# VectorE's instructions of the state space stage in the order of the kernel's calls

## The chip, the cores and the metric

The kernel runs on one core of one Trainium2 chip. TensorE (PE in the profile) multiplies, VectorE (DVE), ScalarE (ACT) and GpSimd (POOL) do the element-wise work, and transfers are issued from the SyncE queue (SP). The metric is device time in microseconds; lower is better. A difference of less than about 0.2% (5 us) cannot be told from no change here.

## The reference

One layer of a hybrid decoder on 1024 tokens of width 1024: token mixing (stick-breaking attention beside a Mamba-2 mixer), cross-attention into 256 memory tokens, and a SwiGLU feed-forward. Float32 data are carried as a high and a low part, and a product is three matmuls (high x high, high x low, low x high). The part that matters here is the state space mixer, in chunks of 128 tokens, with 32 heads in 4 groups:

```python
cb = einsum('bclgn,bcsgn->bcgls', cc, bc)
y_diag = einsum('bcgls,bcgels,bcsgep->bclgep', cb, decay, xc)
states = einsum('bclgn,bcgel,bclgep->bcgepn', bc, decay_to_end, xc)
# scan over chunks: prev * chunk_decay + states
y_off = einsum('bclgn,bcgepn,bcgel->bclgep', cc, prev_states, exp(a_cs))
y = (y_diag + y_off + d_skip * x) * silu(z)      # then an RMS norm within each group
```

The result goes through the projection `w_br_ssm`. In the same stretch of the program the keys and values of the cross-attention are computed from the memory tokens, since nothing else depends on them yet.

## The kernel before

The kernel is written for a framework that schedules. Python calls create instructions; a planner then chooses, for each engine, the order in which that engine will run them, by the data they need and its own guess of durations. On the chip every engine runs its own list strictly from the front, and waits on semaphores of the others. So the order of calls is not the order on an engine, unless code says so. `InTurn` wraps an engine and can say so: while its `on` is set, each instruction of that engine is planned behind the one created before it. It is in use in two other stretches of the kernel (`lead_in`). In the state space stage it is off.

The stage is a loop over 32 chunk steps `n` (4 groups `g` of 8 chunks `c`), preceded by two steps that only prepare. In one turn of the loop the calls are, in this order:

- `prep(n + 2)`: every fourth chunk `open_four` splits B and C (tiles `bl`, `cl` on VectorE, L122) and masks their product (`cb`, L1114). Then for the chunk: two matmuls into `dec` (L1137), two exponentials on ScalarE (L1138), one wide multiply by `cb` on VectorE (tile `seg`, L1139), and the weighted x: a multiply on GpSimd (L1144), its high part on ScalarE and its low part on VectorE (`s2r`, L122).
- `branch_load`: in four of the eight steps of a group, a block of `w_br_ssm` is scaled and split (VectorE's part is L1237, twice).
- `branch`: 12 matmuls of the output projection into a bank `mm`, added to `acc` by VectorE (tile `a`, L1250; ScalarE copies instead for the first group). Up to two of these in a step.
- `states(n + 1)`: three matmuls into `pst`; GpSimd decays the old state (L1161), VectorE adds `pst` (L1162), ScalarE takes the high part `sth`, VectorE the low part `stl` (L122).
- `outp(n)`: GpSimd multiplies x by `dsk` (L1178); three matmuls of C with the state into `po`; VectorE scales `po` (L1183); GpSimd adds it to y (L1184); 16 small matmuls, in two halves, into `pd` (L1191); VectorE adds `pd` (L1194) and multiplies by z (L1195); ScalarE squares (L1198), GpSimd makes the reciprocal root (L173, L174), ScalarE scales (L1200).
- `flip(n - 2)`: four transposes into `ptr` (L1213), ScalarE takes the high part (L1216), VectorE the low part `otl` (L1217).

Between these calls `mem_work` spreads the memory work (64 small pieces) over the first eight turns: 16 weight blocks are loaded and split (VectorE's part is tile `bw`, L122, 128x1024), and the matmuls of a block come after the load of the block two ahead. Room for the split blocks is two tiles `bw` of two blocks each, so the fifth block waits until the products of the first two are done.

PSUM has one bank each for `pst`, `po`, `pd` and `ptr`, and two each for `dec` and `mm`: TensorE can run about one step ahead of VectorE and no further.

Of the kernel before, what the change touches and what calls it, by code (L numbers as in the profile page):

```python
# [54 lines left out]
def hybrid_block(ctx, tc, a, out, dbg=None):  # L55
    nc = tc.nc
    V, A, T = [InTurn(tc, e) for e in (nc.vector, nc.scalar, nc.tensor)]
# [12 lines left out]
    def mk(pl, shape, dt, tag, bufs=None):  # L70
        uid[0] += 1
        kw = {} if bufs is None else {"bufs": bufs}
        return pl.tile(shape, dt, tag=tag, name=f"{tag}_{uid[0]}", **kw)
# [50 lines left out]
    def mm3(ps, sh, sl, mh, ml, start, stop):  # L124
        first = T.matmul(ps, sh, mh, start=start, stop=False)  # L125
        T.matmul(ps, sh, ml, start=False, stop=False)  # L126
        T.matmul(ps, sl, mh, start=False, stop=stop)  # L127
        return first
# [874 lines left out]
    with ExitStack() as p3:  # L1003
# [146 lines left out]
        def states(n):  # L1150
            g, c = divmod(n, NCH)
            d, gd = chk[n], grp[g]
            if c == NCH - 1:
                return
            pst_ = mk(ps, [P, HALF], F32, "pst")
            marks.append(mm3(pst_, d["bh"], d["bl"], d["xwh"], d["xwl"], True, True))
            state = mk(gb, [P, HALF], F32, "state")
            if c == 0:
                A.activation(state, pst_, AF.Copy)
            else:  # L1160
                G.tensor_tensor(v3(state), v3(gd["state"]), bc(cdm, c, g), ALU.mult)  # L1161
                V.tensor_tensor(state, state, pst_, ALU.add)  # L1162
            gd["state"] = state
            sth = mk(gb, [P, HALF], F32R, "sth")
            stl = mk(gb, [P, HALF], F32R, "stl")
            hi_sb(sth, state, "a")
            lo_of(stl, state, sth)
            gd["st", c + 1] = (sth, stl)
# [34 lines left out]
        def flip(n):  # L1203
            g, c = divmod(n, NCH)
            half, ci = divmod(c, 4)
            gd = grp[g]
            if ci == 0:
                gd["oh", half] = mk(ot, [P, 4, HALF], F32R, "oth")
                gd["ol", half] = mk(ot, [P, 4, HALF], F32R, "otl")
            y = chk[n]["y"]  # L1210
            pt = mk(ps, [P, 4, P], F32, "ptr")
            for k in range(4):
                T.transpose(pt[:, k, :], y[:, k * P:(k + 1) * P], ident)  # L1213
            sl = slice(ci * P, (ci + 1) * P)
            oh = gd["oh", half][:, :, sl]
            A.activation(oh, pt, AF.Copy)  # L1216
            V.tensor_tensor(gd["ol", half][:, :, sl], pt, oh.bitcast(F32), ALU.subtract)  # L1217
# [7 lines left out]
        def branch_load(g, fh, kk):  # L1225

            if (g, fh) not in brw:
                brw[g, fh] = halves()
            w = brw[g, fh]
            raw = mk(wr, [P, 2, HALF], F32, "wraw")  # L1230
            r0 = g * HALF + kk * 2 * P
            nc.sync.dma_start(raw, a["w_br_ssm"][0][r0:r0 + 2 * P, fh * HALF:(fh + 1) * HALF].rearrange("(k p) f -> p k f", p=P))
            for j in range(2):
                k = 2 * kk + j
                gain = pcol("g_ssm_norm", g * 4 + k)
                A.activation(w[:, k, 0], raw[:, j], AF.Copy, scale=gain)
                V.scalar_tensor_tensor(w[:, k, 1], raw[:, j], gain, w[:, k, 0].bitcast(F32), ALU.mult, ALU.subtract)  # L1237

        def branch(g, half, f):
            oh, ol = grp[g]["oh", half], grp[g]["ol", half]  # L1240
            sl = slice(half * HALF, (half + 1) * HALF)
            w = brw[g, f // 4]
            fs = slice(f % 4 * P, (f % 4 + 1) * P)
            pb = mk(ps, [P, HALF], F32, "mm", bufs=2)
            for k in range(4):
                mm3(pb, w[:, k, 0, fs], w[:, k, 1, fs], oh[:, k, :], ol[:, k, :], k == 0, k == 3)
            if g == 0:
                A.activation(acc[f][:, sl], pb, AF.Copy)
            else:
                V.tensor_tensor(acc[f][:, sl], acc[f][:, sl], pb, ALU.add)  # L1250
# [4 lines left out]
        def mem_quanta():  # L1255
# [63 lines left out]
            for i, ps_ in enumerate(parts):  # L1319
                if i + 2 < len(loads):  # L1320
                    yield loads[i + 2]
                yield from ps_

        for n in range(AHEAD):
            prep(n)
        mq = list(mem_quanta())
# [2 lines left out]
        def mem_work(upto):  # L1329
            while mq and NQ - len(mq) < upto:  # L1330
                mq.pop(0)()
# [8 lines left out]
        for n in range(-AHEAD, NN + 2):  # L1340
            if AHEAD <= n + AHEAD < NN:
                prep(n + AHEAD)
            mem_work((n + AHEAD) * NQ / MEM_SPAN)
            for l in loads.pop(n, []):
                branch_load(*l)
            if todo and todo[0][0] <= n:
                todo.pop(0)[1]()
            if 0 <= n + 1 < NN:
                states(n + 1)
            mem_work((n + AHEAD + 0.33) * NQ / MEM_SPAN)  # L1350
            if 0 <= n < NN:
                outp(n)
            mem_work((n + AHEAD + 0.67) * NQ / MEM_SPAN)
            if todo and todo[0][0] <= n:
                todo.pop(0)[1]()
            if 0 <= n - 2 < NN:
                flip(n - 2)
                if (n - 2) % 4 == 3:
                    g, c = divmod(n - 2, NCH)
                    fs = list(range(KT)) if c == 3 else list(range(4, KT)) + list(range(4))  # L1360
                    todo += [(n + 2, lambda g=g, hf_=c // 4, f=f: branch(g, hf_, f)) for f in fs]

# [889 lines left out]
```

## Time and profile before

| | |
|---|---|
| median of 3 runs | 2514.5 us (2513.93 to 2516.95) |
| the profiled execution | 2516.72 us, of which the span is 2515.0 us |
| busy: TensorE, VectorE, ScalarE, GpSimd | 2449.4, 1803.6, 1161.5, 720.2 us |
| state space stage | from about 1086.6 to 1411 us of the span |
| in it, busy: TensorE, VectorE | 311.12 and 281.58 of 324.40 us |

An engine that is busy throughout sets the time of its stretch, if its work is not itself stretched by waits; here TensorE is nearly always busy, and VectorE is nearly so in the early part of the stage. Timeline rows give the start, the duration, the engine, the line and the operation, and in brackets the idle time just ahead and what ended it. An instruction of VectorE shows some 0.08 us more than the distance to the start of the next, since two of them overlap at their ends.

### The profile page before, as it was taken

The numbers are of one execution on the slowest core, as the hardware profiler recorded it, in microseconds if no ns is written. First come the engines' busy times: TensorE is split into PE (matmuls) and PEld (weight loads), VectorE is DVE, ScalarE is ACT, GpSimd is POOL, SyncE is SP. The second block draws the span as 40 slices with busy tenths as digits, with TensorE's granted clock in tenths as the row PEclk, the third lists the DMA queues.
The fourth block names the chain that finished last, engine by engine and source line by source line (L and its number), as shares of the span: only waits on it lengthen the run. The fifth ranks groups of instructions, "written<-read, shape, count | busy, mean of one in ns | idle before, by whom it ended". The sixth has DMA issues, their size and how long they took to land. (4 is left out here: it accounts for less than half of the span.)

```text
span 2515.0 us, 33312 instructions
## 1 busy us (share of the span) xinstructions
PE 2449.4 (97%) x12306; PEld 2016.7 (80%) x12306; DVE 1803.6 (72%) x2205; ACT 1161.5 (46%) x2054; POOL 720.2 (29%) x581
## 2 busy tenths in 40 slices
PE   7999999999999999999999999999999999999998
PEld 5788888888877888877777787887888888888887
DVE  7665777767587878689888674577368665666997
ACT  5333455555555665566644312344335333344433
POOL 3221545443111111146666241104011332220001
PEclk9999999999999999999999999999999999999999
DMA  7431443333534343366333481322142322234322
GB/s 248 157 118 49 138 145 107 109 101 93 160 97 109 95 117 91 94 191 206 98 100 88 136 273 64 131 94 67 67 151 63 101 80 76 93 98 165 131 101 101
DMA packets 249132, 295.62 MB, mean 118 GB/s; under 512 B 17023, under 2 KB 169096, under 8 KB 248842
## 3 DMA queue, kind: packets, MB, share of 16 engines
q1 hardware_dynamic: 248682, 292.45, 36.9%
q8 instruction: 97, 1.59, 0.3%
q10 hardware_dynamic: 288, 1.05, 0.1%
q14 instruction: 65, 0.53, 0.1%
HBM read 202.20 MB, written 74.45 MB: 110 GB/s over the span
## 5 line engine op out<-in xcount | busy, mean ns | idle before, releaser
L911 DVE TENSOR_TENSOR_SCAN n<-n,mask 128x128 f32<-128x128 f32 (+7 forms) x128 | 189.8, 1510 | 23.7 <-ACT n L910 22.4
L122 DVE TENSOR_TENSOR sw<-sf,sw 128x512 fp32r<-128x512 f32 x142 | 129.5, 916 | 69.6 <-ACT sw L119 67.6
L119 ACT ACTIVATE sw<-sf 128x512 fp32r<-128x512 f32 x142 | 88.9, 628 | 155.8 <-PE mm L230 139.2
L928 ACT ACTIVATE wth<-tr,mone 128x512 fp32r<-128x512 f32 x192 | 110.7, 585 | 83.6 <-PE tr L925 81.7
L929 DVE SCALAR_TENSOR_TENSOR wtl<-tr,wth 128x512 fp32r<-128x512 f32 x192 | 99.7, 544 | 48.6 <-ACT wth L928 48.6
L693 DVE SCALAR_TENSOR_TENSOR b<-b,prmT,b 128x1023 f32<-128x1023 f32 (+2 forms) x72 | 109.7, 1523 | 16.9 <-ACT b L687 16.3
L196 POOL TENSOR_TENSOR sf<-wr,wr 128x512 f32<-128x512 f32 x36 | 51.8, 1438 | 232.7 <-DMA wr<-in_w_gu_dram 95.1
L122 DVE TENSOR_TENSOR sw<-wr,sw 128x512 fp32r<-128x512 f32 x107 | 100.3, 939 | 24.4 <-ACT sw L119 24.3
L229 PE MATMUL mm<-h,sw 128*128 128x512 f32 x288 | 112.0, 389 | 0.0
L230 PE MATMUL mm<-h,sw 128*128 128x512 f32 x288 | 111.7, 389 | 0.0
L228 PE MATMUL mm<-h,sw 128*128 128x512 f32 x288 | 109.9, 389 | 0.0
L910 ACT ACTIVATE n<-sc 128x512 f32<-128x512 f32 (+1 forms) x192 | 88.6, 494 | 45.9 <-PE tr L925 28.7
L173 POOL TENSOR_SCALAR rstd<-ms 128x1 f32<-128x1 f32 x74 | 29.3, 396 | 273.9 <-ACT x L180 195.0
L125 PE MATMUL mm<-oth,bw 128*128 128x512 f32 x256 | 103.7, 405 | 3.1 <-DVE a L1250 3.1
L115 POOL TENSOR_SCALAR v<-va 128x512 fp32r<-128x512 f32 x16 | 20.5, 1282 | 286.3 <-PE av L938 166.3
L127 PE MATMUL p<-bw,h 128*128 128x512 f32 x256 | 100.2, 392 | 0.5 <-DVE h L122 0.5
L127 PE MATMUL mm<-oth,bw 128*128 128x512 f32 x256 | 100.5, 393 | 0.0
L126 PE MATMUL mm<-otl,bw 128*128 128x512 f32 x256 | 100.5, 392 | 0.0
L125 PE MATMUL p<-bw,h 128*128 128x512 f32 x256 | 99.9, 390 | 0.0
L126 PE MATMUL p<-bw,h 128*128 128x512 f32 x256 | 99.8, 390 | 0.0
L925 PE MATMUL tr<-ident,n 128*128 128x128 f32 x576 | 95.5, 275 | 3.6 <-DVE wtl L929 3.6
L119 ACT ACTIVATE zh<-zr 128x512 fp32r<-128x512 f32 x72 | 45.0, 630 | 104.8 <-PE ma L492 52.4
(661 smaller groups left out, 7814.2 us busy)
## 6 DMA issues: line engine op xcount, KB each, us to landing
wr<-in_w_in_dram SPq DMA_DIRECT2D x36, 512.0 KB
wr<-in_w_gu_dram SPq DMA_DIRECT2D x72, 256.0 KB
zr<-in_w_in_dram SPq DMA_DIRECT2D x28, 512.0 KB
wraw<-in_w_in_dram SPq DMA_DIRECT2D x20, 512.0 KB
gu_d<-t SPq DMA_DIRECT2D x36, 256.0 KB
zs_d<-zo SPq DMA_DIRECT2D x32, 256.0 KB
xs_d<-b SPq DMA_DIRECT2D x32, 256.0 KB
kl<-gt SPq DMA_DIRECT2D x64, 128.0 KB
```

Of the source, the lines that this page charges most:

```text
L119: A.activation(o, i, AF.Copy)
L122: eng.tensor_tensor(o, i, hi.bitcast(F32), ALU.subtract)
L125: first = T.matmul(ps, sh, mh, start=start, stop=False)
L126: T.matmul(ps, sh, ml, start=False, stop=False)
L127: T.matmul(ps, sl, mh, start=False, stop=stop)
L228: T.matmul(ps, w[0][:, k, :], bh, start=first and k == 0, stop=False, skip_group_check=True)
L229: T.matmul(ps, w[0][:, k, :], bl, start=False, stop=False, skip_group_check=True)
L230: ins = T.matmul(ps, w[1][:, k, :], bh, start=False, stop=last and k == 3, skip_group_check=True)
L693: V.scalar_tensor_tensor(acc[:, sh:], y[:, :S - sh], cw(3 - sh, f), acc[:, sh:], ALU.mult, ALU.add)
L911: V.tensor_tensor_scan(nt[:, 0:L][:, ::-1], nt[:, 0:L][:, ::-1], mask[:, S - L:][:, ::-1], 1.0, ALU.mult, ALU.max)
L928: A.activation(wh[:, t0 * P:], pt[:, t0 * P:], AF.Identity, bias=mone)
L929: V.scalar_tensor_tensor(wl[:, t0 * P:], pt[:, t0 * P:], -1.0, wh[:, t0 * P:].bitcast(F32), ALU.add, ALU.subtract)
```

## The change

VectorE's wrapper is switched on for the whole stage. All its instructions of `prep`, `mem_work`, `branch_load`, `branch`, `states`, `outp` and `flip` now stand on VectorE in the order of the calls. Nothing is computed otherwise, and no instruction is added; the planner places the other engines' instructions anew around the fixed list.

```diff
+        V.on = True
         for n in range(AHEAD):
             prep(n)
         mq = list(mem_quanta())
...
                     todo += [(n + 2, lambda g=g, hf_=c // 4, f=f: branch(g, hf_, f)) for f in fs]
+        V.on, V.last = False, None
```

Inside the wrapper an instruction carries the wrapper's line (L49) instead of its own.

The first place is VectorE in an ordinary step of the last group, before. `s4` is the tile of `seg`, `s2_2830` the scaled `po` and `s2_2828` the y of the same chunk.

```order
L1139 SCALAR_TENSOR_TENSOR s4_2816_13323<-s4_2816_13323,cb_2768_13113 128x1024
L1250 TENSOR_TENSOR a8_2050_9940<-a8_2050_9940,mm_2822_13337 128x512
L1162 TENSOR_TENSOR state_2824_13355<-state_2824_13355,pst_2823_13351 128x512
L1183 TENSOR_TENSOR s2_2830_13370<-po_2829_13366,eam_428_2335 128x512
L122 TENSOR_TENSOR stl_2826_13359<-state_2824_13355,sth_2825_13358 128x512
L1194 TENSOR_TENSOR s2_2828_13364<-s2_2828_13364,pd_2831_13373 128x512
L1195 TENSOR_TENSOR s2_2828_13364<-s2_2828_13364,s2_2827_13362 128x512
```

The same place on VectorE now:

```order
L49 SCALAR_TENSOR_TENSOR s4_2816_13323<-s4_2816_13323,cb_2768_13113 128x1024
L49 TENSOR_TENSOR s2r_2821_13334<-s2_2819_13331,s2r_2820_13333 128x512
L49 TENSOR_TENSOR a8_2050_9940<-a8_2050_9940,mm_2822_13337 128x512
L49 TENSOR_TENSOR state_2824_13355<-state_2824_13355,pst_2823_13351 128x512
L49 TENSOR_TENSOR stl_2826_13359<-state_2824_13355,sth_2825_13358 128x512
L49 TENSOR_TENSOR s2_2830_13370<-po_2829_13366,eam_428_2335 128x512
L49 TENSOR_TENSOR s2_2828_13364<-s2_2828_13364,pd_2831_13373 128x512
L49 TENSOR_TENSOR s2_2828_13364<-s2_2828_13364,s2_2827_13362 128x512
```

`stl`, which needs ScalarE's answer to `state`, now stands directly behind `state`; the scaled `po`, to which GpSimd answers, stands behind `stl` and directly ahead of the add of `pd` that needs GpSimd's answer.

The second place is VectorE at the start of the stage, before. `bw` are the split memory weights (`bw_2097` blocks 1 and 2, `bw_2100` blocks 3 and 4, `bw_2111` block 5), `s2_2129` is the y of the first chunk.

```order
L122 TENSOR_TENSOR stl_2108_10165<-state_2106_10162,sth_2107_10164 128x512
L1139 SCALAR_TENSOR_TENSOR s4_2115_10212<-s4_2115_10212,cb_2082_10074 128x1024
L1194 TENSOR_TENSOR s2_2129_10271<-s2_2129_10271,pd_2130_10273 128x512
L122 TENSOR_TENSOR s2r_2120_10223<-s2_2118_10220,s2r_2119_10222 128x512
L1195 TENSOR_TENSOR s2_2129_10271<-s2_2129_10271,s2_2128_10269 128x512
L122 TENSOR_TENSOR bw_2100_10121<-wraw_2104_10154,bw_2100_10121 128x1024
L1162 TENSOR_TENSOR state_2122_10242<-state_2122_10242,pst_2121_10238 128x512
L122 TENSOR_TENSOR s2r_2141_10335<-s2_2139_10332,s2r_2140_10334 128x512
L122 TENSOR_TENSOR bw_2111_10196<-wraw_2112_10197,bw_2111_10196 128x1024
```

The same place on VectorE now:

```order
L49 TENSOR_TENSOR bw_2100_10121<-wraw_2104_10154,bw_2100_10121 128x1024
L49 TENSOR_TENSOR stl_2108_10165<-state_2106_10162,sth_2107_10164 128x512
L49 TENSOR_TENSOR bw_2111_10196<-wraw_2112_10197,bw_2111_10196 128x1024
L49 SCALAR_TENSOR_TENSOR s4_2115_10212<-s4_2115_10212,cb_2082_10074 128x1024
L49 TENSOR_TENSOR s2r_2120_10223<-s2_2118_10220,s2r_2119_10222 128x512
L49 TENSOR_TENSOR state_2122_10242<-state_2122_10242,pst_2121_10238 128x512
L49 TENSOR_TENSOR stl_2124_10246<-state_2122_10242,sth_2123_10245 128x512
L49 TENSOR_TENSOR bw_2111_10196<-wraw_2126_10258,bw_2111_10196 128x1024
L49 TENSOR_TENSOR s2_2129_10271<-s2_2129_10271,pd_2130_10273 128x512
```

The first half of `bw_2111`, whose room comes free only with the products of the first two blocks, has moved ahead of the third `s4`, its `s2r`, the state and the first chunk's y.

## The prediction

> **What bounds the kernel now.** I read the busy shares of the page first, then the busy time by stretches of the stage, then the timeline of one ordinary step, then VectorE's waits.
>
> ```profile
> PE 2449.4 (97%) x12306; PEld 2016.7 (80%) x12306; DVE 1803.6 (72%) x2205; ACT 1161.5 (46%) x2054; POOL 720.2 (29%) x581
> ```
>
> Over the whole program TensorE is the bound. The change touches one stage only, so the four groups of that stage are taken apart; the stretches are cut at the first chunk's end of each group. Columns: length, then busy time and instructions of TensorE, its weight loads, VectorE, ScalarE, GpSimd, then the granted clock, the DMA share and GB/s.
>
> ```profile
> 1086.60:1193.00 106.40, 99.06 (x752) 80.83 (x752) 97.34 (x104) 68.37 (x121) 62.19 (x50) 0.97 0.67 208
> 1193.00:1272.00 79.00, 77.18 (x572) 62.53 (x571) 62.84 (x78) 45.95 (x90) 49.29 (x47) 1.00 0.35 104
> 1272.00:1348.00 76.00, 74.30 (x557) 60.01 (x557) 68.34 (x90) 38.72 (x75) 45.41 (x44) 1.00 0.36 106
> 1348.00:1411.00 63.00, 60.57 (x465) 48.81 (x465) 53.05 (x73) 28.18 (x54) 33.73 (x35) 1.00 0.27 76
> 1086.60:1411.00 324.40, 311.12 (x2342) 252.18 (x2342) 281.58 (x341) 181.22 (x340) 190.62 (x174) 0.99 0.44 133
> ```
>
> In the last three groups TensorE is busy 96 to 98%, in the first (memory work) 93%, with VectorE at 91%. TensorE leaves 13.3 us of 324.4 unused, VectorE 42.8 us. So there is little to gain, and VectorE has 42.8 us to lose before it becomes the bound, as long as its waits fall where TensorE still has work.
>
> How much of that is left within a step is seen in one ordinary step, from one multiply by z to the next (VectorE), with GpSimd and TensorE beside it:
>
> ```profile
> 1376.85 0.80 DVE L1195 TENSOR_TENSOR s<-s,s 128x512 f32<-128x512 f32 x1
> ...
> 1381.64 0.68 DVE L1162 TENSOR_TENSOR state<-state,pst 128x512 f32<-128x512 f32 x1
> 1382.23 0.69 DVE L1183 TENSOR_TENSOR s<-po,eam 128x512 f32<-128x512 f32 x1
> 1383.08 0.91 DVE L122 TENSOR_TENSOR stl<-state,sth 128x512 fp32r<-128x512 f32 x1 [0.16 <-ACT sth L119]
> 1385.16 0.69 DVE L1194 TENSOR_TENSOR s<-s,pd 128x512 f32<-128x512 f32 x1 [1.18 <-PE dec L1137]
> 1385.89 0.91 DVE L1195 TENSOR_TENSOR s<-s,s 128x512 f32<-128x512 f32 x1
> ```
>
> ```profile
> 1382.39 1.04 POOL L1161 TENSOR_TENSOR state<-state,cdm 128x512 f32<-128x512 f32 x1 [2.35 <-DVE state L1162]
> 1383.40 1.73 POOL L1184 TENSOR_TENSOR s<-s,s 128x512 f32<-128x512 f32 x1
> ```
>
> ```profile
> 1380.37 1.15 PE L1191 MATMUL pd<-s,s 128*64 128x64 f32 x32
> ...
> 1389.42 0.98 PE L1191 MATMUL pd<-s,s 128*64 128x64 f32 x26
> ```
>
> TensorE's period is 1389.42 - 1380.37 = 9.05 us, VectorE's 1385.89 - 1376.85 = 9.04 us. Within it VectorE sits idle for 0.16 us ahead of `stl` and 1.18 us ahead of the add of `pd`. The row names a matmul for the second, but GpSimd's L1184 ended at 1385.13, 0.03 us before the add began, and the add reads its output: that is the true releaser. This step hides two round trips in each other. After `state`, ScalarE makes `sth`; in that time VectorE scales `po`. GpSimd then adds the scaled `po` while VectorE makes `stl`.
>
> **The change, part by part.** It removes and adds no arithmetic and no transfer. It moves instructions on VectorE, with four effects.
>
> First, the round trip to ScalarE. `stl` now stands right behind `state`. From the rows above, `state` began at 1381.64 and `stl` could begin at 1383.08, 1.44 us later, since ScalarE's part took until then. Without the 0.68 us of `state` itself, VectorE is idle for 0.76 us where it scaled `po` before. There are 24 such states.
>
> Second, the round trip to GpSimd. The scaled `po` now stands directly ahead of the add of `pd`, and nothing of VectorE lies between. The trace has this situation once, at the end of the stage:
>
> ```profile
> 1407.14 0.68 DVE L1183 TENSOR_TENSOR s<-po,eam 128x512 f32<-128x512 f32 x1
> ...
> 1407.90 1.29 POOL L1184 TENSOR_TENSOR s<-s,s 128x512 f32<-128x512 f32 x1 [1.45 <-DVE s L1183]
> ...
> 1409.22 0.69 DVE L1194 TENSOR_TENSOR s<-s,pd 128x512 f32<-128x512 f32 x1 [1.40 <-POOL s L1184]
> ```
>
> 2.08 us from start to start, and 1.40 us of it idle. There are 28 such chunks:
>
> ```profile
> L1183 DVE TENSOR_TENSOR s<-po,eam 128x512 f32<-128x512 f32 x28 | 19.1, 683 | 0.1
> L1162 DVE TENSOR_TENSOR state<-state,pst 128x512 f32<-128x512 f32 x24 | 16.3, 678 | 0.0
> ```
>
> GpSimd's add has two prices in the trace: 1.73 us at 1383.40, where `stl` ran on VectorE until 1383.99, and 1.29 us at 1407.90, where VectorE stood still. In the new order VectorE stands still during it, so I take 1.29; with 1.73 the idle time would be 1.84 us, and the sum 28 x 0.44 = 12.3 us more. The Trainium skill's page "SBUF — State Buffer", section "Who interferes with whom", says why the two may differ: a VectorE instruction with two SBUF inputs contends with a GpSimd instruction that reads SBUF, and the later one is blocked until the first is through. `stl` is such an instruction, and the rows agree in direction (0.44 us more, for 0.59 us of overlap), so by that rule too the lower price holds where VectorE waits.
>
> Put into the ordinary step: `state` to the add of `pd` took 1385.16 - 1381.64 = 3.52 us. Now it is 1.44 (state to `stl`) + 0.84 (`stl`, 0.91 us less the overlap with the next) + 2.08 = 4.36 us. The step becomes 9.04 + 0.84 = 9.88 us, above TensorE's 9.05. Here the bound changes: TensorE has one bank for each of `pst`, `po`, `pd` and `ptr`, so it can run ahead by about a step and then waits for VectorE.
>
> The stage then takes, in each group, VectorE's busy time plus the waits that it can no longer fill. A group has 7 scaled `po` and 6 added states: 7 x 1.40 + 6 x 0.76 = 14.4 us.
>
> First group: 97.34 + 14.4 = 111.7 against 106.4 us: +5.3. Second: 62.84 + 14.4 = 77.2 against 79.0; TensorE's 77.18 us of work lie under it, so I leave it at 79: 0. Third: 68.34 + 14.4 = 82.7 against 76.0: +6.7. Fourth: 53.05 + 14.4 = 67.4 against 63.0: +4.4. Together +16.4 us.
>
> Third, the other waits of VectorE. They are these now, longest total first (total, times, longest):
>
> ```profile
> DVE s L1194 <- POOL s L1184: 14.7, 11, 2.8
> DVE s L1139 <- ACT s L1138: 8.0, 9, 3.1
> DVE s2r L122 <- ACT s2r L119: 7.7, 9, 1.8
> DVE bw L122 <- ACT bw L119: 5.1, 4, 2.1
> DVE otl L1217 <- ACT oth L1216: 3.8, 4, 1.8
> DVE bw L1237 <- ACT bw L1236: 1.6, 2, 1.4
> DVE s L1194 <- PE dec L1137: 1.2, 1, 1.2
> DVE stl L122 <- ACT sth L119: 0.9, 6, 0.2
> DVE bl L122 <- ACT bh L119: 0.3, 1, 0.3
> ```
>
> The first, the seventh and the eighth (16.8 us) are the two round trips, counted above. The other six sum to 26.5 us: exponentials, high parts, weight splits. A list in fixed order cannot go round them, but the longer step also gives ScalarE and TensorE more time, and `s2r` now stands last in a step, far behind GpSimd's part. So they lie between 0 and, in the three groups where VectorE becomes the bound, three quarters of 26.5, some 20 us. I take the middle, 10 us (an estimate).
>
> Fourth, at the start the first half of `bw_2111` waits for room, until the products of the first two weight blocks are done. Behind it on VectorE stand the third `s4`, its `s2r`, `state` and `stl`, and behind those wait TensorE's `pst` and `pd`. One line of a block's products is in the groups of TensorE's instructions:
>
> ```profile
> L127 PE MATMUL mm<-mh,bw 128*128 128x256 f32 x64 | 18.5, 289 | 1.1 <-DVE bw L122 1.1
> ```
>
> A block has three such lines of 8, so at most 24 x 0.289 = 6.9 us, less what is pipelined and what VectorE's own splits ahead of it cover: between 0 and 7 us. I take it as inside the 10 us above, since TensorE is at work in that wait, and keep 5 us for the upper end.
>
> SP's and GpSimd's lists shift with the buffers that VectorE frees, but no transfer is added and the DMA share is 0.27 to 0.36 in the last three groups, so I cost that at nothing; if a load of x came late, it would show as a longer wait of GpSimd's L1144. After the stage nothing changes: the last products and adds of `branch` follow in the same order.
>
> The sum: 16.4 + 10 = +26 us on the profiled execution, 2516.7 to about 2543. That execution lies 2.2 us above the median of 2514.5 us, so the median becomes 2540.5 us.
>
> **The rivals.** *TensorE's clock falls.* When TensorE waits long enough, its next products run slower. The trace shows it once, in the first group:
>
> ```profile
> 1164.21 0.80 PE L126 MATMUL mm<-bw,mh 128*128 128x512 f32 x1 [1.78 <-DVE bw L122]
> ...
> 1165.23 0.63 PE L125 MATMUL mm<-bw,mh 128*128 128x512 f32 x1
> 1165.66 0.63 PE L126 MATMUL mm<-bw,mh 128*128 128x512 f32 x1
> ...
> 1167.72 0.39 PE L126 MATMUL mm<-bw,mh 128*128 128x512 f32 x1
> 1167.95 0.40 PE L127 MATMUL mm<-bw,mlo 128*128 128x512 f32 x1
> ```
>
> After a wait of 1.78 us the starts are 0.43 us apart instead of 0.23 for about 3 us: some 1.5 us lost beside the wait. Another wait did not do it:
>
> ```profile
> 1361.97 0.50 PE L1137 MATMUL dec<-colrows,keyrows 128*128 128x512 f32 x1 [1.29 <-ACT s L1138]
> ```
>
> So this rival decides from a single wait somewhere between 1.3 and 1.8 us. Against it: an ordinary step makes TensorE wait 9.88 - 9.05 = 0.83 us. For it: steps with `open_four` or `branch_load` put three to four more instructions on VectorE's list, and what TensorE waits for them comes in one piece. Once in each of the 24 steps with a state it costs 24 x 1.5 = 36 us on top of 26: about 2576. The Trainium skill's page "TensorE: Matmul & The Clock Gate", section "What's actually happening", has a stricter rule: the half clock comes after at least one idle window of about 3.4 us. By that rule hardly any step would fall into it and the sum would stay at 26 us; the row above shows it after a shorter single wait, and the row decides.
>
> *Faster: the call order stops VectorE from running ahead.* In the first group the planner lets VectorE split weights and prepare `bl` and `cl` of later chunks before work that TensorE needs; TensorE then stood idle for 106.40 - 99.06 = 7.3 us there, and 13.3 us in the whole stage. If call order brought each TensorE input just in time, and VectorE's waits fell where it has slack, all of that could go: 2514.5 - 13 = 2501. It decides for the faster side only if the ordinary step stays at or below 9.05 us, which means that GpSimd's answer must come 0.83 us sooner than the rows say. I see nothing that would bring it.
>
> *No difference.* VectorE's 42.8 us of idle time swallow the new waits in the groups with slack, and the second group's surplus is used. It would take the 16.4 us to be no more than 5.
>
> *The change does nothing* can be left out: the lists of VectorE in both places shown differ.
>
> **How the numbers follow.** VectorE becoming the bound, with a loss of more than 5 us and up to about 55: 0.67. The clock rival: 0.11. No difference within 0.2% (5 us, what can be told here): 0.10. Faster by more than 5 us: 0.12. Slower is 0.67 + 0.11 = 0.78. The forecast's own upper end is 16.4 + 20 + 12.3 + 5 = 54 us, so 2568; its lower end is near no change. The range reaches below to 2512, which leaves most of the faster case out, and above to 2578, which takes in most of the clock case.
>
> **What would show it.** In the changed kernel's profile: the add of `pd` waiting for GpSimd's L1184, now under the wrapper's line, near 28 x 1.40 = 39 us instead of 14.7; a wait on `sth` near 24 x 0.76 = 18 us instead of 0.9; GpSimd's L1184 near 1.29 us instead of 1.73; an ordinary step in the last two groups of about 9.9 us; TensorE's idle time in the stage up by roughly the time lost, in pieces below 1.3 us. I am wrong if TensorE's step stays at 9.05 us, if GpSimd's add does not get shorter, if the six other waits grow instead of halving, or if the granted clock in the stage falls clearly below 0.99.

## The result, and the profile after

The changed kernel takes 2546.4 us (median of 4 runs, 2542.4 to 2548.5) against 2514.8 us for the kernel before (median of 4): a ratio of 1.0119, with a 95% interval from 1.0105 to 1.0133. It is slower by some 30 us; the forecast was 26. Its profiled execution took 2546.62 us, of which the span is 2544.9 us.

The page of the changed kernel, busy shares over the whole program:

```profile
PE 2453.7 (96%) x12306; PEld 2016.7 (79%) x12306; DVE 1780.5 (70%) x2205; ACT 1162.6 (46%) x2054; POOL 719.6 (28%) x581
```

VectorE is busy for 23 us less than before, in a program that is 30 us longer. The stage, cut at the same chunks as in the table of before (columns as there):

```profile
1086.60:1212.50 125.90, 107.29 (x779) 87.79 (x779) 86.78 (x101) 69.61 (x124) 57.67 (x51) 0.94 0.54 167
1212.50:1288.50 76.00, 72.56 (x546) 57.55 (x545) 57.15 (x78) 45.13 (x88) 47.08 (x45) 0.98 0.37 113
1288.50:1373.20 84.70, 75.78 (x557) 59.38 (x556) 64.93 (x91) 39.28 (x75) 45.47 (x44) 1.00 0.30 95
1373.20:1440.50 67.30, 62.13 (x459) 48.98 (x458) 50.30 (x74) 27.78 (x53) 35.86 (x35) 0.97 0.27 77
```

The groups are longer by 19.5, -3.0, 8.7 and 4.3 us, 29.5 us in all. VectorE's busy time fell from 281.6 to 259.2 us and its idle time rose from 42.8 to 94.7 us: +52 - 22.4 = 29.5. In the third group TensorE, which was idle for 1.7 us of 76.0, is now idle for 8.9 of 84.7. Over the stage TensorE's idle time rose from 13.3 to 36.1 us and its busy time from 311.1 to 317.8 us, with six matmul records fewer: 22.9 us more of waiting, and 6.6 us more for the same products at a lower granted clock (0.97 over the stage, 0.99 before).

VectorE's waits over the stage (total, times, longest):

```profile
DVE s L49 <- POOL s L1184: 40.6, 28, 1.9
DVE stl L49 <- ACT sth L119: 36.9, 24, 3.2
DVE bw L49 <- ACT bw L119: 8.0, 3, 4.1
DVE bw L49 <- ACT bw L1236: 4.6, 2, 2.4
```

The two round trips hold 77.5 of the 94.7 us. One ordinary step of the last group on VectorE, from one multiply by z to the next:

```profile
1394.56 0.80 DVE L49 TENSOR_TENSOR s<-s,s 128x512 f32<-128x512 f32 x1
...
1398.80 0.68 DVE L49 TENSOR_TENSOR state<-state,pst 128x512 f32<-128x512 f32 x1
1400.69 0.69 DVE L49 TENSOR_TENSOR stl<-state,sth 128x512 fp32r<-128x512 f32 x1 [1.21 <-ACT sth L119]
...
1403.38 0.69 DVE L49 TENSOR_TENSOR s<-s,pd 128x512 f32<-128x512 f32 x1 [1.40 <-POOL s L1184]
1404.11 0.80 DVE L49 TENSOR_TENSOR s<-s,s 128x512 f32<-128x512 f32 x1
```

The step takes 9.55 us. Both trips stand bare in it, one behind the other. The longest wait of this kind stands one step later, which has a block of `w_br_ssm` to split; VectorE's rows, then ScalarE's in the same time:

```profile
1408.36 0.67 DVE L49 TENSOR_TENSOR state<-state,pst 128x512 f32<-128x512 f32 x1
1412.21 0.69 DVE L49 TENSOR_TENSOR stl<-state,sth 128x512 fp32r<-128x512 f32 x1 [3.18 <-ACT sth L119]
```

```profile
1408.61 2.56 ACT L1236 ACTIVATE bw<-wraw,prmT 128x512 fp32r<-128x512 f32 x4 [0.19 <-PE mm L127]
...
1411.56 0.61 ACT L119 ACTIVATE sth<-state 128x512 fp32r<-128x512 f32 x1
```

The state was there from 1409.03 on, but ScalarE's own list has four weight parts and the transposed y ahead of `sth`. VectorE stands still until ScalarE gets there.

Most of the loss lies in the first group. VectorE at its start:

```profile
1104.30 1.23 DVE L49 TENSOR_TENSOR bw<-wraw,bw 128x1024 fp32r<-128x1024 f32 x1 [2.96 <-ACT bw L119]
...
1110.18 1.22 DVE L49 TENSOR_TENSOR bw<-wraw,bw 128x1024 fp32r<-128x1024 f32 x1 [4.05 <-ACT bw L119]
...
1117.35 0.68 DVE L49 TENSOR_TENSOR s<-s,pd 128x512 f32<-128x512 f32 x1
```

ScalarE's high parts that these two splits wait for, and the loads on SP's queue:

```profile
1103.21 1.06 ACT L119 ACTIVATE bw<-wraw 128x1024 fp32r<-128x1024 f32 x1 [0.48 <-DMA wraw<-in_w_xkv_dram]
...
1109.08 1.06 ACT L119 ACTIVATE bw<-wraw 128x1024 fp32r<-128x1024 f32 x1 [0.88 <-DMA wraw<-in_w_xkv_dram]
```

```profile
1099.42 0.39 SPq L1266 DMA_DIRECT2D wraw<-in_w_xkv_dram  x1
1102.26 0.32 SPq L1289 DMA_DIRECT2D kT_d<-wraw  x1
...
1104.89 0.40 SPq L1266 DMA_DIRECT2D wraw<-in_w_xkv_dram  x1
```

The list's head waits for blocks of the memory weights whose loads are issued at 1099.42 and 1104.89 and land some 4 us later; between the two issues a finished memory product is written out (`kT_d`). Behind it stands the first chunk's add of `pd`, though TensorE had done its products by 1092.3 and GpSimd its multiply of x by 1096.3. That add begins at 1117.35; before, at 1104.48.

To compare kernels whose earlier stages ended at slightly different times, I use two stretches: from the last copy of the stage before (ScalarE, tile `oT`) to the add of `pd` of the third group's first chunk, and from there to the add of the last chunk. The last copy and the first of the two adds, before and then after; the last adds are at 1409.22, a row of the prediction, and at 1438.75:

```profile
1085.03 0.60 ACT L941 ACTIVATE oT<-av 128x512 f32<-128x512 f32 x1 [0.93 <-PE av L938]
1271.78 0.67 DVE L1194 TENSOR_TENSOR s<-s,pd 128x512 f32<-128x512 f32 x1
```

```profile
1083.31 0.60 ACT L941 ACTIVATE oT<-av 128x512 f32<-128x512 f32 x1 [1.49 <-PE av L938]
1288.48 0.68 DVE L49 TENSOR_TENSOR s<-s,pd 128x512 f32<-128x512 f32 x1
1438.75 0.69 DVE L49 TENSOR_TENSOR s<-s,pd 128x512 f32<-128x512 f32 x1 [1.41 <-POOL s L1184]
```

The first stretch grew from 186.75 to 205.17 us (+18.4), the second from 137.44 to 150.27 (+12.8). The stretches come from one execution of each kernel, so a difference of a few us in them carries little weight: executions of the kernel before differ by up to 10 us over the whole program. All kernels in this measure, each less the kernel before, with the ratio of times and its 95% interval:

| kernel | first two groups, us | last two groups, us | ratio to before |
|---|---|---|---|
| changed | +18.4 | +12.8 | 1.0119 (1.0105 to 1.0133) |
| scaled `po` between `state` and `stl` | +18.2 | -0.1 | 1.0072 (1.0060 to 1.0085) |
| memory splits not in the list | +4.0 | +11.1 | 1.0064 (1.0051 to 1.0077) |
| only `states` and `outp` in order | -1.5 | -1.6 | 0.9994 (0.9985 to 1.0003) |
| order in the first turns only | +17.3 | +0.1 | 1.0068 (1.0055 to 1.0081) |
| both parts undone | +0.8 | +0.5 | 1.0003 (0.9994 to 1.0013) |
| memory splits one block later | +23.1 | +11.1 | 1.0135 (1.0119 to 1.0152) |
| `sth` on VectorE | +15.5 | +9.4 | 1.0099 (1.0084 to 1.0114) |
| add of scaled `po` on VectorE | +14.4 | -0.2 | 1.0058 (1.0045 to 1.0071) |
| memory products through the s tiles | +16.5 | +10.4 | 1.0111 (1.0095 to 1.0126) |
| splits not in the list, add on VectorE | -2.0 | -1.2 | 0.9990 (0.9981 to 0.9999) |
| both parts undone, products through s tiles | -4.1 | +0.6 | 0.9989 (0.9980 to 0.9998) |
| before, products through s tiles | -1.8 | -0.4 | 0.9994 (0.9985 to 1.0002) |

### The profile page after: what moved, and what is told of

The parts are those of the page before. It is cut to its first block, busy times and chain, and to the rows that moved or that the text cites. A ratio compares the mean times of both kernels' runs of the same rounds, so it can differ in the third digit from the quotient of the medians.

```text
span 2544.9 us, 33262 instructions
## 1 busy us (share of the span) xinstructions
PE 2453.7 (96%) x12306; PEld 2016.7 (79%) x12306; DVE 1780.5 (70%) x2205; ACT 1162.6 (46%) x2054; POOL 719.6 (28%) x581
## 5 line engine op out<-in xcount | busy, mean ns | idle before, releaser
L693 DVE SCALAR_TENSOR_TENSOR b<-b,prmT,b 128x1023 f32<-128x1023 f32 (+2 forms) x72 | 109.2, 1517 | 16.4 <-ACT b L687 15.8
L119 ACT ACTIVATE sw<-wr 128x512 fp32r<-128x512 f32 x107 | 67.1, 628 | 56.0 <-PE mm L230 50.9
```

The lines of the kernel that those rows point to most:

```text
L119: A.activation(o, i, AF.Copy)
L693: V.scalar_tensor_tensor(acc[:, sh:], y[:, :S - sh], cw(3 - sh, f), acc[:, sh:], ALU.mult, ALU.add)
```

## The experiments

All start from the changed kernel, except the last. The theory is the prediction's: VectorE in fixed order stands still in round trips, becomes the bound, and each group takes its busy time plus its waits. The rivals are the start of the stage, and the fixed list as such.

**The pair turned round.** `outp` is split; its first half (loads, `po`, L1183, GpSimd's add) is called between the state and its low part.

```diff
-            lo_of(stl, state, sth)
...
+            if 0 <= n < NN:
+                outp_po(n)
+            if 0 <= n + 1 < NN:
+                low_state(n + 1)
...
             if 0 <= n < NN:
                 outp(n)
```

> VectorE's list stays fixed; only the pair is turned round, so that the scaled po stands between state and stl as before the change: state, scaled po, stl, add of pd. Theory (the two round trips stand bare in the new order, 40.6 us on GpSimd's and 36.9 us on ScalarE's answer): both trips lie in each other again, the wait for GpSimd falls below 20 us and that for sth below 20 us, GpSimd's add goes back towards 1.7 us, and the stage gets back 15 to 24 us, about 2523 to 2531 us. Rival 1 (the cost is the start of the stage, where the memory weights' splits hold up the list): at most 5 us come back, 2541 to 2546 us. Rival 2 (any fixed list of VectorE costs this much, by waits for whatever comes late): waits fall in these two rows and as much grows in others, 2540 to 2546 us.

```profile
DVE s L49 <- POOL s L1189: 24.9, 15, 3.2
DVE stl L49 <- ACT sth L119: 20.5, 18, 3.4
```

Ratio 1.0072 against 1.0119: 0.47%, some 12 us, came back. The two waits (L1189 is GpSimd's add here) fell from 77.5 to 45.4 us; the theory had both below 20. The gain is a little under the theory's 15 to 24 us, and it lies in one place only: the last two groups are whole again (-0.1), the first two are as late as ever (+18.2). So the order of the pair is the whole cost of the last two groups; in the first two, turning it gains nothing as long as the weight splits stand in the list.

**Memory splits left out of the list.**

```diff
         def mem_work(upto):
+            V.on = False
             while mq and NQ - len(mq) < upto:
                 mq.pop(0)()
+            V.on = True
```

> Only the splits of the memory weights (16 blocks in the first group) are left out of the fixed list; everything else on VectorE stays in call order. Theory (round trips): the first group keeps its 7 bare round trips, so of its +19.5 us at most the part that the trips do not explain comes back, 8 to 14 us, about 2532 to 2538 us, and the last three groups keep their +10 us. Rival 1 (the start of the stage is the cost): the first group returns to about what it was, 17 to 20 us come back, about 2527 us. Rival 2 (neither; the list as such): no change, 2543 to 2548 us.

```profile
1086.60:1196.10 109.50, 98.80 (x775) 82.80 (x775) 88.19 (x99) 68.03 (x123) 59.33 (x51) 1.00 0.62 189
```

Ratio 1.0064: 0.55%, 14 us came back, the top of the theory's range; the time alone doesn't decide. The table does: the first two groups go from +18.4 to +4.0, the last two keep +11.1. The first group's row (stretch to the first chunk of the second group) is 109.5 us instead of 125.9, and the granted clock 1.00 instead of 0.94. VectorE's list holds the same pairs there. The memory splits at its head are thus a second cause, as large as the first.

**Only the pair in order.** The call order binds VectorE inside `states` and `outp`, nowhere else.

```diff
-        V.on = True
         for n in range(AHEAD):
...
             if 0 <= n + 1 < NN:
+                V.on = True
                 states(n + 1)
+                V.on = False
...
             if 0 <= n < NN:
+                V.on = True
                 outp(n)
+                V.on = False
```

> The call order binds VectorE only inside the two calls states and outp (state, stl, scaled po, add of pd, multiply by z); weight splits, masks, low parts of x, products' adds and otl may be put between them or elsewhere. Theory (round trips): where nothing is put between, the trips stay bare; the planner can fill some of them, so the time lies between the kernel before and the changed one, 2520 to 2538 us, with the waits for sth and for GpSimd's add together at 30 to 70 us instead of 77.5. Rival 1 (start of the stage): the lag of the first group goes, the others keep theirs: about 2527 us with the two waits still near 77 us. Rival 2 (call order of all the other work is what costs): 2515 to 2518 us with the two waits unchanged.

```profile
DVE s L49 <- POOL s L1184: 20.9, 19, 1.4
DVE stl L49 <- ACT sth L119: 10.0, 12, 1.4
```

```profile
1290.00:1370.00 80.00, 78.18 (x577) 62.84 (x576) 68.67 (x94) 38.57 (x76) 47.40 (x47) 1.00 0.32 94
```

The waits are 30.9 us, as the theory allowed, but the time is that of the kernel before (0.9994), which only the second rival had forecast, though with the waits unchanged: the theory's 2520 to 2538 us was missed. `stl` still stands directly behind `state` in 10 of 24 cases and the add of `pd` directly behind the scaled `po` in 9 of 28; each wait for `sth` is shorter (0.83 us instead of 1.54), and the planner puts other work between the rest. In the stretch from 1290 to 1370 TensorE is busy for 78.2 of 80 us, with VectorE at 68.7. Bare trips cost nothing here, since VectorE with its waits still keeps up with TensorE. That they cost in the changed kernel because all the rest of the list is fixed too fits this, but is not shown apart from the smaller number of bare pairs.

**Order in the first turns only.**

```diff
         for n in range(-AHEAD, NN + 2):
+            if n == 6:
+                V.on, V.last = False, None
```

> The call order binds VectorE only in the first turns of the loop, while memory work is still there; from turn 6 on the planner is free as before the change. Theory (round trips, wherever they stand bare): the last three groups lose their +10 us, the first keeps most of its +19.5 us (it has 6 of the 28 pairs, and the memory work): 2530 to 2537 us. Rival 1 (the start of the stage alone): all of the first group's lag stays and is carried to the end, 2534 us, and with it the low clock (0.94) in the first group. Rival 2 (the lag at the start is taken up later by TensorE's slack): near 2515 to 2522 us.

Ratio 1.0068, +17.3 us in the first two groups, +0.1 in the last two. Theory and first rival had forecast nearly the same time here; the second rival falls: what is lost at the start is not taken up later, since TensorE has almost no slack there.

**Both parts undone.** The edits of the first two experiments together.

> Both parts undone together: the splits of the memory weights are left out of the fixed list, and the scaled po stands between state and stl again; the rest of VectorE stays in call order. By the two runs before, freeing the splits took back 17.4 us at the start (lag of the first add of pd 0.3 instead of 12.9 us, lag after 16 chunks 1.0 instead of 16.7) and turning the pair took back some 12 us in the last two groups. Theory (two separate causes that add up): 0 to 6 us above the kernel before, with its first chunk not late and no lag growing in the last two groups. Rival 1 (one cause, seen from two sides): 10 to 15 us above. Rival 2 (a third cost of the fixed list remains, the other waits of VectorE): 6 to 10 us above, with waits for exponentials or low parts grown.

Ratio 1.0003 (0.9994 to 1.0013): no difference from before. The two causes roughly add up (14 and 12 us by themselves, 29 together), and the rest of VectorE in call order costs nothing that can be measured.

**Memory splits one block later.** Each split is called with the load of the next block.

```diff
                 hi_sb(hi, raw, "a")
-                lo_of(lo, raw, hi)
+                if st.get("due"):
+                    lo_of(*st["due"])
+                st["due"] = lo, raw, hi
...
```

> As the changed kernel, but each memory block's split on VectorE is called one block later, together with the load of the next block; the list is still fixed. In the changed kernel VectorE waits 2.96 and 4.05 us at 1104.30 and 1110.18 for ScalarE's high part of a block whose load was issued at 1099.42 and 1104.89, after VectorE itself had freed a raw buffer. Theory (a split at the head of VectorE's list waits for a load that only VectorE's own earlier split let start): the waits of bw for ScalarE fall from 12.6 to below 4 us and the first group gets back 8 to 15 us, so 15 to 23 us above the kernel before. Rival 1 (the room of the split blocks, two tiles of two blocks, is what the list waits for): no change, 28 to 33 us above. Rival 2 (a raw buffer is now held longer, so loads start later): 30 to 38 us above with longer waits for bw.

```profile
DVE stl L49 <- ACT sth L119: 39.1, 24, 3.5
DVE bw L49 <- ACT bw L1236: 11.0, 2, 5.8
DVE bw L49 <- ACT bw L119: 1.6, 1, 1.6
```

VectorE's waits for memory blocks (the last row) fell from 8.0 to 1.6 us, but those for blocks of `w_br_ssm` rose from 4.6 to 11.0, and the ratio is 1.0135: the time is the second rival's. Its interval meets that of the changed kernel, so it is shown that nothing came back, not that more was lost. The waiting moved, for `sth` too. ScalarE's own list has the high part of a memory block directly ahead of `sth`:

```profile
1108.12 1.06 ACT L119 ACTIVATE bw<-wraw 128x1024 fp32r<-128x1024 f32 x1 [0.86 <-DMA wraw<-in_w_xkv_dram]
1109.08 0.62 ACT L119 ACTIVATE sth<-state 128x512 fp32r<-128x512 f32 x1
```

Now ScalarE waits for the load, and VectorE, in its fixed order, for ScalarE (2.75 us at 1109.73 in this trace). Moving one instruction in the list did not help.

**Memory products copied out through other buffers.** The raw blocks keep their three buffers to themselves.

```diff
-                        o = mk(wr, [P, D], F32, "wraw")[:, :ML]
+                        o = mk(t2, [P, HALF], F32, "s2")[:, :ML]
...
-                        o = mk(wr, [P, D], F32, "wraw")[:, :HALF]
+                        o = mk(t2, [P, HALF], F32, "s2")[:, :HALF]
```

> As the changed kernel, but the memory products (keys and values) are copied out through the buffers of the s tiles, not through those of the raw weight blocks. In the changed kernel the fifth block's load is issued at 1104.89, only after the first product's copy (ScalarE, 1101.85) was written out and its buffer came free, and VectorE stands before this block's split from 1106.13 to 1110.18. Theory (the list's head waits for a load that waits for a raw buffer, not for the room of the split blocks): the fifth block's load is issued near 1099.5, its split on VectorE starts 3 to 4 us earlier, and with the blocks after it 4 to 12 us of the 17 us at the start come back: 19 to 27 us above the kernel before. Rival 1 (the room of the split blocks): the load comes earlier but the split still starts near 1110, 28 to 33 us above. Rival 2 (the products' copies now hold up the s tiles, and with them the loads of x and z): 33 to 40 us above, with longer waits of GpSimd's multiplies.

In this trace the stage before ends at 1089.29, 5.98 us later than in the changed kernel. VectorE's split of the fifth block, SP's load of it, and GpSimd's weighted x:

```profile
1110.49 1.23 DVE L49 TENSOR_TENSOR bw<-wraw,bw 128x1024 fp32r<-128x1024 f32 x1 [1.63 <-ACT bw L119]
```

```profile
1103.63 0.39 SPq L1266 DMA_DIRECT2D wraw<-in_w_xkv_dram  x1
```

```profile
1114.21 1.05 POOL L1144 TENSOR_TENSOR s<-s,wm 128x512 f32<-128x512 f32 x1 [10.44 <-DMA s<-xs_d]
```

Less the 5.98 us the load is issued at 1097.7, 7.2 us earlier than 1104.89, and the split starts at 1104.5, 5.7 us earlier than 1110.18. So the split had waited for its load, and the load for a buffer that held a product; the room of the split blocks was not the last to come. But the ratio is 1.0111: GpSimd stood idle for 10.4 us until its next x had landed in an s tile, and VectorE for 3.1 us behind it. The mechanism of the theory is shown for this one wait, and its price is not: the edit brought a wait of its own.

**The trips taken away one by one.**

```diff
-            hi_sb(sth, state, "a")
+            hi_sb(sth, state, "v")
```

> As the changed kernel, but the high part sth of the state is taken by VectorE itself, so that stl waits for no other engine: 36.9 us of waits go, 28 copies of 128x512 come, at no more than the 0.61 us from start to start of such an instruction, 17 us in all. Theory (the bare round trips cost where VectorE is the bound, in the last two groups, 12 us for both trips together): half of the trips' cost or a little less comes back, 3 to 8 us, so 23 to 28 us above the kernel before; the start of the stage stays as late as it is. Rival 1 (the trip to ScalarE is the larger one because other work stands ahead of sth on ScalarE's list, 1.54 instead of 0.76 us each): 8 to 14 us come back, 17 to 23 us above. Rival 2 (VectorE's list is short of time, not of answers): the copies cost what the waits did, 29 to 34 us above.

```diff
-                G.tensor_tensor(y, y, yo, ALU.add)
+                V.tensor_tensor(y, y, yo, ALU.add)
```

> As the changed kernel, but VectorE itself adds the scaled po to y, so that the add of pd waits for no other engine: 40.6 us of waits go, 28 adds of 128x512 come, at 0.61 us from start to start 17 us in all. In an ordinary step 1.40 us of idle time become 0.61 us of work: 0.79 us less. Theory (bare round trips cost in the last two groups alone, where the step had grown by 0.83 us): 15 to 16 steps x 0.79, some 12 us come back, 18 to 21 us above the kernel before. Rival 1 (the trips do not matter, the start of the stage does): 28 to 33 us above. Rival 2 (in every group): 28 x 0.79 = 22 us come back, 8 to 12 us above.

With `sth` on VectorE: 1.0099, 5 us back, the theory's range, though its interval still meets that of the changed kernel. With the add on VectorE: 1.0058, 15 us back, between the theory's 12 and the second rival's 22: the last two groups are whole (-0.2) and 4 us come back in the first two. An ordinary step of that kernel on VectorE:

```profile
1382.90 0.85 DVE L49 TENSOR_TENSOR s<-s,s 128x512 f32<-128x512 f32 x1
...
1390.25 0.74 DVE L49 TENSOR_TENSOR s<-s,s 128x512 f32<-128x512 f32 x1
...
1391.82 0.85 DVE L49 TENSOR_TENSOR s<-s,s 128x512 f32<-128x512 f32 x1
```

Its step is 8.92 us, below TensorE's 9.05 us of before: the trip to ScalarE may stand bare once the other is gone (27.9 us of waits for `sth` are left). VectorE does 28 more adds there, and the kernel is faster for it.

**Three versions that could beat both kernels.** Memory splits out of the list with the add on VectorE; both parts undone with the products through the s tiles; and the kernel before with the products through the s tiles.

> As the changed kernel, with the memory weights' splits out of the fixed list and the add of the scaled po on VectorE. The first took back 14 us by itself, the second 16 us by itself (ratios 1.0064 and 1.0058 against 1.0119). Theory (two separate causes): they add up, -2 to +4 us against the kernel before. Rival 1 (they overlap in the first group, where both VectorE waits lie): 4 to 10 us above. Rival 2 (28 more adds make VectorE late where its list is still free for splits): 10 us above or more.

> The version with both parts undone (memory weights' splits free, scaled po between state and stl; 1.0003 of the kernel before), and with the memory products copied out through the s tiles. If loads of raw blocks hold up the first group there as well, 2 to 5 us come back against the kernel before (TensorE was idle for 7.3 us in its first group). If the first group is bound by TensorE and the other waits, no difference beyond 2.5 us. If the s tiles become short, 3 to 8 us slower.

> The kernel before, with only the memory products copied out through the s tiles, nothing fixed on VectorE. Same three cases as the run before it: 2 to 5 us faster if the loads of raw blocks hold up the first group (TensorE waited 1.78 us for a split of bw there, and ran at a granted clock of 0.91 between 1160 and 1180 us); within 2.5 us if TensorE's work is the bound; 3 to 8 us slower if the s tiles become short.

0.9990, 0.9989 and 0.9994, or 2.5, 2.8 and 1.5 us less than before. The first confirms once more that the two causes are separate. The second lies in its forecast for loads that hold up the first group (2 to 5 us), the third in that for no difference: what the loads of raw blocks hold up is too little to be told from nothing. The best is 0.11% under the kernel before, with an interval up to 0.9998: less than the 0.2% that I call a difference. TensorE's work is the bound again (in the second it is busy for 306.6 of the stage's 320.7 us), and no fixed order that was tried gains on the planner's.

## Why the prediction was right, and where it was off

*VectorE becomes the bound, and a group takes its busy time plus its waits: right.* Third group: 84.7 us, forecast 82.7; fourth: 67.3, forecast 67.4; both are whole again once the scaled `po` fills the one trip, or VectorE's own add replaces the other. Second: 76.0 us, left at 79 in the forecast. TensorE's longest totals of waiting from 1290 to the end of the stage now name VectorE's tiles:

```profile
PE pd L1191 <- DVE s L49: 4.7, 5, 1.1
PE mm L125 <- DVE a L49: 3.9, 8, 1.2
PE dec L1137 <- ACT s L1138: 3.3, 1, 3.3
```

Before, VectorE's tiles had 1.1 us from 1275 on. TensorE's idle time rose by 22.9 us against 29.5 lost, so the bound is VectorE's, but not all pieces are below 1.3 us as forecast: the last row is a single wait, and the first group has seven of 1.5 to 2.5 us.

*The trip to GpSimd: right.* 40.6 us of waits, forecast 39; 1.40 us in the step shown. GpSimd's add is down from 1.73 us in the step shown of before to the lower price, as VectorE stands still:

```profile
L1184 POOL TENSOR_TENSOR s<-s,s 128x512 f32<-128x512 f32 x28 | 36.1, 1289 | 55.2 <-DVE s L49 55.2
```

*The trip to ScalarE: mis-sized.* 36.9 us, forecast 18; 1.54 instead of 0.76 us each. I priced `sth` as if ScalarE were free. Its list has weight parts, exponentials and `oth` ahead of it.

*VectorE's busy time as in before: off the other way.* It fell by 22.4 us. The group in which the difference is largest, before and after:

```profile
L122 DVE TENSOR_TENSOR stl<-state,sth 128x512 fp32r<-128x512 f32 x28 | 31.5, 1126 | 1.0 <-ACT sth L119 0.9
```

```profile
L49 DVE TENSOR_TENSOR stl<-state,sth 128x512 fp32r<-128x512 f32 x28 | 22.0, 787 | 36.9 <-ACT sth L119 36.9
```

9.5 us less for the same work. In the changed kernel 19 of the 28 subtracts ran while GpSimd stood still, and took 676 to 693 ns; the other nine, with GpSimd at work beside them, took 930 to 1099 ns. Before, GpSimd was at work beside all 28. The groups that read a PSUM tile did not change (`state` 678 and 677 ns, the scaled `po` 683 and 682). So where engines wait for one another they no longer get in each other's way. The ordinary step is 9.55 us for that reason, not 9.88: `state` to the add of `pd` takes 4.58 us (forecast 4.36), the rest 4.97 instead of 5.52. This error and the one before nearly cancel (some 19 us more of waiting for `sth`, 22.4 us less of work). That the sum came within some 5 us of the loss is in part luck. The Trainium skill's page "SBUF — State Buffer", section "Who interferes with whom", has the exclusive lock between the two engines; the rows agree in direction on both sides of it, and I had used it on GpSimd's side alone.

*The six other waits: between 0 and 20 us, taken as 10.* 14.2 of the 26.5 us are left, and of these 12.6 are the weight splits. That exponentials and low parts would cost little was right.

*The start: the step that failed.* I gave the first group +5.3 us and a part of the 10, and the wait at the start 0 to 7 us as a wait for room. The group lost 19.5 us. The two waits are 7.0 us long, the upper end, but they are for loads; and they were only the first of it. TensorE's waits for `bw` in this group rose from 3.2 to 10.3 us, and VectorE waited for `sth` behind ScalarE's blocks (1.87 us at 1115.61). TensorE's longest total there:

```profile
PE mm L126 <- DVE bw L49: 7.0, 4, 2.5
```

Freeing the splits gives 14 us back, where I had put the start inside the 10 us of all other waits; turning the pair gives 12 back, where I had 16.4 for the two trips. Which single resource sets the remaining pace of that group stays open: the two attempts to take away one of its waits each brought another.

*The rival of the falling clock: in part.* It fell to 0.94 in the first group, by little or nothing in the others (0.98, 1.00, 0.97), and over the stage from 0.99 to 0.97, which was one of my signs of being wrong. The sum had this at nothing. The rival's own price, 1.5 us once in each step with a state, did not come either: the third group has 1.00. TensorE in the first group:

```profile
1096.04 0.50 PE L125 MATMUL pst<-s2r,bh 128*128 128x512 f32 x1 [2.32 <-ACT state L1159]
...
1098.23 0.42 PE L126 MATMUL mm<-mlo,bw 128*128 128x256 f32 x1
1098.44 0.41 PE L127 MATMUL mm<-mh,bw 128*128 128x256 f32 x1
```

Two us after a wait of 2.32 us has ended, the starts go to 0.21 us apart, for some 3 us (1098.02 to 1101.22), then back to 0.12. The Trainium skill's page "TensorE: Matmul & The Clock Gate", section "What's actually happening", puts the half clock after an idle window of about 3.4 us; no single wait around this row was that long, as in the row of before.

My own reading, that a single wait of between 1.3 and 1.8 us decides, is wrong too. The kernel before has a wait of 1.82 us in its second group, and the changed kernel the one of 3.27 us in its third, which ends at 1307.71:

```profile
1247.18 0.50 PE L1137 MATMUL dec<-colrows,keyrows 128*128 128x512 f32 x1 [1.82 <-DVE cb L1114]
```

After both, the products of `mm` start 0.23 us apart, the full pace, and both groups have a granted clock of 1.00. From 1410 to 1420 of the changed kernel the clock is 0.83 with no single wait above 1.12 us. So the length of one wait does not decide, and what does stays open.

Taking the clock's shortfall in the four groups as lost time, 125.9 x 0.06 + 76.0 x 0.02 + 67.3 x 0.03 - 106.4 x 0.03 = 7.9 us of the 29.5 are the clock's, 4.4 of them in the first group (an estimate; TensorE's busy time rose by 6.6). With the splits freed, the first group's row has 1.00 again.

*Faster by call order* was wrong for the reason given: the ordinary step did not stay below 9.05 us.

## What to carry to other kernels

When a list is fixed in call order, look at each pair in it whose second member needs another engine's answer to the first: what used to stand between them is the price, and it falls due only where the engine's work and waits together exceed those of the engine that was the bound. Price the answer by what stands ahead of it on the answering engine's own list, not by the operation alone. And look first for list entries that wait for a transfer, since everything behind them waits too: here 16 weight splits cost 14 us, and 52 round trips 12.

## What the runs showed of the hardware that I had not expected

Contention between VectorE and GpSimd is worth most of the 22 us by which VectorE's busy time fell in this stage, three quarters of what the whole change cost. The fall lies in the groups that read two SBUF tiles: `stl` 9.5 us, `seg` 5.8, `s2r` 5.7, the splits of B and C 2.5. VectorE's subtract `stl` took 1126 ns on the mean in the kernel before and 787 ns in the changed one, GpSimd's add 1.73 us beside VectorE and 1.29 us alone. Giving VectorE 28 adds of GpSimd's (0.74 us in the step shown) saved 15 us in the changed kernel, since GpSimd's answer had cost 40.6 us of standing still, 1.45 us each time.

TensorE's clock does not follow the length of a single wait: products ran at about half pace after waits of 1.78 and 2.32 us, and at full pace after waits of 1.82 and 3.27 us.
